# A second layer's dense width of 158 instead of 160, with the two tokens between as a gathered set of their own

## The chip, the cores and the metric

The kernel runs on one core of a Trainium2 chip. The metric is the device time of one execution in microseconds. A measurement gives the times of several runs and their median, and one more execution is recorded by the hardware profiler. Its trace counts from the first instruction to the last; that stretch is called the span.

The engines are called as the profile calls them: PE is TensorE (matmuls; PEld is its weight load), DVE is VectorE, ACT is ScalarE, POOL is GpSimd, SP is SyncE. DMA transfers are issued from queues of SP, ACT and POOL and carried by 16 DMA engines.

## The reference

The program is a trunk of two layers over 256 tokens of 1024 numbers. A layer first mixes tokens (projections, attention, convolution, gating) and then runs a retrieval over 16,384 single-neuron experts, which is what the change touches:

```python
q = (t @ w_pq).reshape(T, PEER_HEADS, 2, PEER_HALF)
...                                   # two top-16 searches over 128 keys, then 16 of the pairs per head
u = expert_down[experts]              # 8 heads x 16 = 128 rows of 1024 per token
act = gelu(einsum('td,thkd->thk', t, u))
wgt = gate * act
vv = expert_up[experts]               # the same 128 rows of the other table
y = einsum('thk,thkd->td', wgt, vv)
```

Each token uses 128 of the 16,384 experts. Both tables are 64 MB of float32 for each layer.

## The kernel before

**Two ways for a token.** For the first T tokens of a layer the kernel does not gather. It multiplies the whole table with them: the down table goes through PE in 128 chunks of 128 experts (8 matmuls of 128x128 weights by T columns each, L403), gives the dots of all experts with all T tokens, and these are masked by a matrix of gates that is zero where a token did not pick an expert. The up table then goes through PE in the same 128 chunks (L1225), into four PSUM banks named `acc`. These are the dense tokens, and T is `DENSE = (168, 160)` for the two layers.

The other TS = 256 - T tokens (88 and 96) are done from gathered rows. One indirect DMA (L1128, POOL) fetches 128 rows of the table, one row of 4 KB to each partition, 512 KB in all; here this is called a row step. A token needs 128 rows, one row step's worth, but the rows of one step belong to several tokens.

**Sets.** The gathered tokens are split into sets of m tokens, m a power of two. In a set of m, partition p holds token p mod m, and the 128 picks of each token are spread over 128/m partitions and m steps. So a set of m tokens needs m steps in the down half and m in the up half, and TS tokens need TS steps in each half, however they are split. `token_sets` gives offset and size of each: 64, 16, 8 in the first layer and 64, 32 in the second. Each set has a 128x1024 tile in `spots`: first its tokens' inputs, repeated over the partitions (`R_DX`), and later its weighted sum of up rows (`R_SUM`). There are four such tiles; those that are no set's serve as staging rows, one of them first holding the inputs before they are spread (`R_DROW`).

**The steps of a set.** `dot_spread` copies the inputs of set 0 into all partitions; `spread_inputs` (L1109) broadcasts those of the other sets from DRAM, 512 KB for each set. `spread_picks` (L1093) brings the picks of set 0 into `pairs`, and `spread_rest` (L1097, L1102) those of the others, two small DMAs for a set. `where` (L1113, DVE) makes row indices of them. Then `fetch` (L1128) issues row steps from POOL as long as a staging row is free; `dot` (L1138, DVE) multiplies a down row with the inputs and sums it, which frees the row for the next `fetch`; `add_row` (L1151 for a set's first row, else L1153, DVE) adds an up row times its weight to the set's sum. At the end `fold_set` (L1233, PE) adds the sums of the 128/m partitions of each token into the columns of `acc` behind the dense ones, eight matmuls for a set with a constant matrix `fold` of m columns. A set that is finished early is folded between chunks, one fold for each of eight chunks, starting 8 chunks after its last add stands in the order (`early_folds`); the last set is folded in and behind the last chunk.

**What sets the order.** From the expert stage on, the program is recorded in the order of the code (`manual_schedule`), so each engine does its instructions in that order and waits where an operand is late. The down loop takes a chunk on PE for each i and hangs the rest on i: gate groups of four tokens (`compare` L1161 on DVE, `factors` L1171 to L1177 on ACT, `gate_mm` L1187 on PE), the row steps, and after a start a fixed rate of dots per chunk (`DOT_RATE`, 0.92 in the second layer). The up loop spreads what is left of the dots and all adds over chunks 4 to 124. The dense weights come on the queues of SP and ACT into a ring of five units of 1 MB, one unit for two chunks; the row steps come on POOL's queue. All three share the 16 DMA engines.

**Rows.** In the second layer the staging rows are one tile of `spots`, the arena at 108, 80 and 84, `R_DROW` from chunk 7, for a time the places of chunks that were loaded ahead, two more after the start, one that is kept, and in the up half four more.

Of the kernel before, what the change touches and what calls it, by code (L numbers as in the profile page):

```python
# [40 lines left out]
PLAN1 = ((5, 'qk_sums k_norm'), (6, 'v_tok'), (7, 'lg10 exp'), (8, 'lg01 lg00 sm00'), (10, 'lg11'), (11, 'sm01 cz'), (12, 'sg'), (13, 'pt00 pt01 sm10 pv0'), (14, 'inv0 ao0 cy pt10'), (15, 'sm11 pt11 inv1 gs4 pv1 as0 ao1 gn4 mix'), (16, 'as1 an0'), (17, 'an1 sqrt'), (20, 'gs6 gn6'))  # L41
G_LAST = 124
OUT_AT = (3, 5, 6, 7)
DENSE = (168, 160)
QUEUE_LAG = 4
PICKS_LAG = 2
LOWER_LAG = 1
# [27 lines left out]

def token_sets(n):

    out, off = [], 0
    for m in (64, 32, 16, 8):
        if n & m:  # L80
            out.append((off, m))
            off += m
    assert off == n and len(out) <= 3
    return out


@with_exitstack
def hybrid_trunk(ctx: ExitStack, tc: tile.TileContext, x_in, c_in, vec_in, w_ada, w_first, w_in, w_out, w_pq,
# [48 lines left out]
    def region(at, *shape):  # L137
        n = 1
        for s in shape:
            n *= s  # L140
        v = flat[:, at:at + n]
        if len(shape) == 2:
            v = v.rearrange("p (a b) -> p a b", b=shape[1])
        elif len(shape) == 3:
            v = v.rearrange("p (a b c) -> p a b c", b=shape[1], c=shape[2])
        return v
# [908 lines left out]
    def experts(layer, rest):  # L1055

        T = DENSE[layer]
        TS = S - T
        SETS = token_sets(TS)
        NG = T // 4  # L1060
        acts = flat[:, :P * T].rearrange("p (i t) -> p i t", t=T)
        R_WHERE, R_DOTS = (region(127 * S, 2, TS)[:, n, :] for n in range(2))
        onehots = {}
        spots = work.tile([P, 4, D], F32, name="spots", tag="hh", bufs=1)
        R_DX = R_SUM = [spots[:, n, :] for n in range(len(SETS))]
        R_DROW = spots[:, 3, :]
        beyond = [region(at * S, D) for at in (80, 84) if at * S >= P * T]
        passing = []
        free = deque([spots[:, n, :] for n in range(len(SETS), 3)] + [region(108 * S, D)] + beyond)
        held = {}  # L1070
# [119 lines left out]

        def gate_use(g, ps, done):
            v = ps.rearrange("p (t i) -> p i t", t=4)
            a = acts[:, :, 4 * g:4 * g + 4]
            if done < 128:
                nc.scalar.activation(a[:, done:], v[:, done:], AF.Copy, scale=1.0 / GATE_SCALE)  # L1195
            if done:
                nc.vector.scalar_tensor_tensor(a[:, :done], a[:, :done], 1.0 / GATE_SCALE, v[:, :done],  # L1197
                                               op0=OP.mult, op1=OP.mult)
# [95 lines left out]
        gdone = 0  # L1294
# [6 lines left out]
        for i in range(128):  # L1301
# [4 lines left out]
            while waiting:  # L1306
                g, gp = waiting.pop(0)
                gate_use(g, gp, 2 * pair)
                gdone = g + 1
            if j == 1:  # L1310
                tdone = 4 * gdone
                pend.append((pair, gelu(pair, ps, tdone), tdone))
                if len(pend) > 1:
                    act_use(*pend.popleft())
# [203 lines left out]
```

## Time and profile before

| what | value |
|---|---|
| median of 3 runs | 1545.63 us (1544.82 to 1546.74) |
| the profiled execution | 1544.97 us |
| its span | 1543.3 us |
| mean granted PE clock | 0.998 |
| second layer's expert stage, down half | about 961 to 1256 us |
| second layer's expert stage, up half | about 1256 to 1537 us |
| HBM read | 563.50 MB |

A row of a timeline reads: start, duration, engine, line, operation, written tile <- read tiles, shapes, count, and in brackets how long the engine stood idle before it and what ended that. PE shows each float32 matmul as two records, so 16 records are one chunk. Durations of matmuls overlap; the distance between the starts is the pace. In the table of stretches each engine has its busy time and, in brackets, its instructions; then come the granted clock, the mean busy share of the 16 DMA engines (it can exceed 1 slightly) and what they moved.

### The profile page before, as it was taken

How to read it: one execution, taken by the hardware profiler on the slowest of the kernel's cores; microseconds unless marked ns; L12 is line 12 of the kernel's file. 1: busy time of each engine (PE TensorE's matmuls, PEld its weight loads, DVE VectorE, ACT ScalarE, POOL GpSimd, SP SyncE). 2: the span in 40 equal slices, each digit the busy share in tenths (PEclk: the TensorE clock that was granted, in tenths of full speed). 3: DMA queues.
4: the chain of work that ended last, by engine and by line, in shares of the span. 5: the costliest groups of instructions: out<-in, count | busy, mean ns of one | idle time of the engine just before them, and what ended most of it. 6: DMA issues, size and time to landing. Idle time of an engine off the chain costs nothing.

```text
span 1543.3 us, 28519 instructions
## 1 busy us (share of the span) xinstructions
PE 1527.7 (99%) x11244; PEld 1494.3 (97%) x11244; DVE 1000.2 (65%) x2249; ACT 478.7 (31%) x1380; POOL 503.2 (33%) x424
## 2 busy tenths in 40 slices
PE   8999999999999999999999999999999999999998
PEld 6879999999999999999999899999999999999998
DVE  7787879677687544444467578797777764443435
ACT  2256322466564000000036663234656620000000
POOL 0000125344334433443300002154344444444542
PEclk9999999999999999999999999999999999999999
DMA  9998299999999999999985573999999999999996
GB/s 387 386 362 319 93 312 380 422 422 422 422 422 420 420 422 423 422 424 423 422 319 169 170 257 107 280 409 423 421 423 423 422 422 423 423 423 423 424 422 283
DMA packets 122120, 570.65 MB, mean 370 GB/s; under 512 B 14292, under 2 KB 14820, under 8 KB 89986
## 3 DMA queue, kind: packets, MB, share of 16 engines
q1 hardware_dynamic: 48818, 240.54, 39.7%
q0 software_dynamic: 55744, 202.36, 32.6%
q10 hardware_dynamic: 17424, 125.93, 19.7%
q8 instruction: 88, 1.44, 0.3%
q14 instruction: 46, 0.38, 0.1%
HBM read 563.50 MB, written 4.09 MB: 368 GB/s over the span
## 4 chain that ended last, share of the span: by engine, by line
PE 84%; DMA 10%; DVE 3%; issue 1%; ACT 1%; POOL 0%; DVEq 0%; ACTq 0%; SPq 0%; POOLq 0%
PE acc L1225 37%; PE ch L403 28%; DMA arena<-in_down_rows,arena 5%; DMA spots<-in_down_rows,arena 3%; PE ch L405 2%; PE ch L406 2%; PE ch L407 2%; PE g L1187 2%; PE ch L494 1%; DVE raw L256 1%; PE g L999 1%; PE acc L405 1%; PE acc L407 1%; PE acc L406 1%; DMA raw<-in_w_ada 1%
## 5 line engine op out<-in xcount | busy, mean ns | idle before, releaser
L1225 PE MATMUL acc<-arena,raw 128*128 128x168 f32 (+1 forms) x4096 | 577.0, 303 | 0.0
L1225 PEld LDWEIGHTS acc<-arena,raw 128*128 128x128 f32 x4096 | 570.8, 190 | 0.0
L403 PE MATMUL ch<-arena,raw 128*128 128x168 f32 (+2 forms) x3808 | 564.3, 307 | 0.6 <-issue 0.6
L403 PEld LDWEIGHTS ch<-arena,raw 128*128 128x128 f32 x3808 | 539.3, 190 | 7.6 <-issue 3.9
L1153 DVE SCALAR_TENSOR_TENSOR spots<-arena,spots 128x1024 f32<-128x1024 f32 x154 | 197.8, 1285 | 263.3 <-DMA arena<-in_up_rows,arena 262.0
L1128 POOL DMA_INDIRECT arena<-in_up_rows,arena x159 | 216.6, 1362 | 283.8 <-DMA arena<-in_up_rows,arena 196.8
L1128 POOL DMA_INDIRECT arena<-in_down_rows,arena x147 | 177.0, 1204 | 223.3 <-DVE arena L1138 177.2
L1138 DVE SCALAR_TENSOR_TENSOR arena<-arena,spots 128x1024 f32<-128x1024 f32 x147 | 177.6, 1220 | 47.8 <-DMA arena<-in_down_rows,arena 46.0
L1171 ACT ACTIVATE arena<-arena,parts 128x128 f16<-128x128 f16 x164 | 64.6, 394 | 107.2 <-DVE arena L1161 85.1
L434 ACT ACT_TABLE_LOAD x6 | 7.7, 1283 | 247.9 <-PE acc L1225 247.8
L405 PE MATMUL ch<-hh,hi 128*128 128x256 f32 x288 | 82.6, 289 | 2.0 <-DVE arena L525 1.9
L406 PE MATMUL ch<-hh,lo 128*128 128x256 f32 x288 | 81.8, 284 | 0.0
L407 PE MATMUL ch<-hh,hi 128*128 128x256 f32 x288 | 81.8, 284 | 0.0
L1204 ACT ACTIVATE arena<-ch 128x336 f32<-128x336 f32 (+32 forms) x122 | 42.1, 346 | 123.7 <-PE ch L403 109.5
L1197 DVE SCALAR_TENSOR_TENSOR arena<-arena,g 128x336 f32<-128x336 f32 (+30 forms) x82 | 40.3, 492 | 49.6 <-ACT arena L1195 47.8
L256 DVE SCALAR_TENSOR_TENSOR raw<-raw,arena 128x1024 f32<-128x1024 f32 x48 | 58.4, 1221 | 12.2 <-DMA raw<-in_w_ada 12.1
L1128 POOL DMA_INDIRECT spots<-in_down_rows,arena x37 | 42.1, 1138 | 73.2 <-DVE spots L1138 54.7
L309 DVE TENSOR_TENSOR lo<-raw,hi 128x1024 fp32r<-128x1024 f32 x42 | 51.1, 1224 | 22.1 <-ACT hi L316 19.2
L1175 ACT ACTIVATE arena<-arena,parts 128x128 f16<-128x128 f16 x164 | 63.4, 387 | 0.0
L1173 ACT ACTIVATE arena<-arena,parts 128x128 f16<-128x128 f16 x164 | 63.4, 386 | 0.0
L1177 ACT ACTIVATE arena<-arena,parts 128x128 f16<-128x128 f16 x164 | 63.4, 386 | 0.0
L403 PE MATMUL ch<-arena 128*128 128x168 f32 (+1 forms) x448 | 63.0, 303 | 0.0
(239 smaller groups left out, 1754.9 us busy)
## 6 DMA issues: line engine op xcount, KB each, us to landing
raw<-in_up SPq DMA_DIRECT2D x64, 1024.0 KB
raw<-in_up ACTq DMA_DIRECT2D x64, 1024.0 KB
raw<-in_down SPq DMA_DIRECT2D x58, 1024.0 KB
raw<-in_down ACTq DMA_DIRECT2D x56, 1024.0 KB
raw<-in_w_ada SPq DMA_DIRECT2D x48, 512.0 KB
aside<-in_w_ada SPq DMA_DIRECT2D x48, 512.0 KB
raw<-in_w_pq SPq DMA_DIRECT2D x32, 512.0 KB
arena<-in_down SPq DMA_DIRECT2D x28, 512.0 KB
```

The lines of the kernel that those rows point to most:

```text
L256: nc.vector.scalar_tensor_tensor(raw, raw, 1.0, cact, op0=OP.mult, op1=OP.mult, accum_out=mods[layer][:, col:col + 1])
L403: nc.tensor.matmul(dst, hi[:, cols], k[0], start=start, stop=stop, **kw)
L405: nc.tensor.matmul(dst, hi[:, cols], k[0], start=start, stop=False, **kw)
L406: nc.tensor.matmul(dst, lo[:, cols], k[0], start=False, stop=False, **kw)
L407: nc.tensor.matmul(dst, hi[:, cols], k[1], start=False, stop=stop, **kw)
L1128: nc.gpsimd.indirect_dma_start(out=held[n], out_offset=None, in_=rows if n >= TS else down_rows[:, :], in_offset=bass.IndirectOffsetOnAxis ...
L1138: nc.vector.scalar_tensor_tensor(row, row, 1.0, R_DX[which(k)[0]], op0=OP.mult, op1=OP.mult, accum_out=R_DOTS[:, k:k + 1])
L1153: nc.vector.scalar_tensor_tensor(R_SUM[s], row, w, R_SUM[s], op0=OP.mult, op1=OP.add)
L1171: nc.scalar.activation(og[0][:, 0, i, :], oh[:, 0, i, :], AF.Copy, scale=parts[:, 0, t + i:t + i + 1])
L1173: nc.scalar.activation(og[1][:, 0, i, :], oh[:, 0, i, :], AF.Copy, scale=parts[:, 1, t + i:t + i + 1])
L1175: nc.scalar.activation(og[0][:, 1, i, :], oh[:, 1, i, :], AF.Copy, scale=parts[:, 0, t + 2 + i:t + 3 + i])
L1225: nc.tensor.matmul(acc[d // 2][:, (d % 2) * S:(d % 2) * S + T], u[:, d * P:(d + 1) * P], acts[:, i, :], start=i == 0 and d % 2 == 0, stop= ...
```

## The change

The second layer's width becomes 158. `token_sets` makes a set of two, if the number of gathered tokens has that bit, and puts it second: 98 tokens become sets of 64, 2 and 32. The first layer's 88 tokens give the same three sets as before. 158 is no multiple of four, so the number of gate groups is rounded up (it stays 40) and the last group uses two of its four columns. The second layer now has three tiles of `spots` as sets and one as `R_DROW`, so that the one that was a staging row from the start is none any more. Its gathered tokens take 98 row steps in each half instead of 96.

```diff
-DENSE = (168, 160)
+DENSE = (168, 158)
...
 def token_sets(n):
 
-    out, off = [], 0
-    for m in (64, 32, 16, 8):
-        if n & m:
-            out.append((off, m))
-            off += m
-    assert off == n and len(out) <= 3
-    return out
+    sizes = [m for m in (64, 32, 16, 8) if n & m]
+    if n & 2:
+        sizes.insert(1, 2)
+    assert sum(sizes) == n and len(sizes) <= 4
+    return [(sum(sizes[:k]), m) for k, m in enumerate(sizes)]
...
-        NG = T // 4
+        NG = -(-T // 4)
...
-        R_DROW = spots[:, 3, :]
         beyond = [region(at * S, D) for at in (80, 84) if at * S >= P * T]
+        R_DROW = spots[:, 3, :] if len(SETS) < 4 else beyond.pop()
...
             v = ps.rearrange("p (t i) -> p i t", t=4)
-            a = acts[:, :, 4 * g:4 * g + 4]
+            a = acts[:, :, 4 * g:min(4 * g + 4, T)]
+            v = v[:, :, :min(4, T - 4 * g)]
...
-                tdone = 4 * gdone
+                tdone = min(4 * gdone, T)
```

The lines of the changed program stand one or two higher than those of the program before. Three places show how the instructions move. The first is POOL at the beginning of the second layer's expert stage: `dot_in` takes the inputs to DRAM, the copies spots<-spots spread set 0, spots<-dot_in are the broadcasts of the other sets, pairs are the picks, and in_down_rows the row steps. Before:

```order
78 L1329 DMA dot_in_112<-spots 96x1024
79 L1088 DMA spots<-spots 64x1024 x2
80 L1109 DMA spots<-dot_in_112 128x1x1024
81 L1093 DMA pairs<-chosen 64x2x64 x2
82 L1128 DMA spots<-in_down_rows,arena 128x1024
83 L1128 DMA arena<-in_down_rows,arena 128x1024 x3
84 L1097 DMA pair_in_110<-chosen 96x256
85 L1102 DMA pairs<-pair_in_110 128x1x32 x2
```

Now:

```order
78 L1328 DMA dot_in_113<-spots 98x1024
79 L1086 DMA spots<-spots 64x1024 x2
80 L1107 DMA spots<-dot_in_113 128x1x1024 x2
81 L1091 DMA pairs<-chosen 64x2x64 x2
82 L1126 DMA arena<-in_down_rows,arena 128x1024 x4
83 L1095 DMA pair_in_111<-chosen 98x256
84 L1100 DMA pairs<-pair_in_111 128x1x2 x2
85 L1100 DMA pairs<-pair_in_111 128x1x32 x2
```

A second broadcast stands ahead of the picks, and two more small DMAs stand ahead of the fifth row step. The second place is DVE at the end of the down half and the beginning of the up half. Before:

```order
1105 L1215 TENSOR_TENSOR arena<-arena 128x320
1106 L1145 TENSOR_TENSOR arena<-arena,pairs 128x95
1107 L1138 SCALAR_TENSOR_TENSOR arena<-arena,spots 128x1024
1108 L1145 TENSOR_TENSOR arena<-arena,pairs 128x1
1109 L1151 TENSOR_SCALAR spots<-arena 128x1024
```

Now:

```order
1104 L1214 TENSOR_TENSOR arena<-arena 128x316
1105 L1143 TENSOR_TENSOR arena<-arena,pairs 128x95
1106 L1136 SCALAR_TENSOR_TENSOR arena<-arena,spots 128x1024 x3
1107 L1143 TENSOR_TENSOR arena<-arena,pairs 128x3
1108 L1149 TENSOR_SCALAR spots<-arena 128x1024
```

95 dots stand in the down half as before, and three in the up half instead of one. The third place is PE at the folds of set 0 in the second layer's up half. Before:

```order
2905 L1225 MATMUL acc<-arena,raw 128x160 x736
2906 L1233 MATMUL acc<-fold_103,spots 128x64
2907 L1225 MATMUL acc<-arena,raw 128x160 x8
2908 L1233 MATMUL acc<-fold_103,spots 128x64
2909 L1225 MATMUL acc<-arena,raw 128x160 x8
2910 L1233 MATMUL acc<-fold_103,spots 128x64
```

Now:

```order
2905 L1224 MATMUL acc<-arena,raw 128x158 x728
2906 L1232 MATMUL acc<-fold_103,spots 128x64
2907 L1224 MATMUL acc<-arena,raw 128x158 x8
2908 L1232 MATMUL acc<-fold_103,spots 128x64
2909 L1224 MATMUL acc<-arena,raw 128x158 x8
2910 L1232 MATMUL acc<-fold_103,spots 128x64
2911 L1232 MATMUL acc<-fold_103,spots 128x2
2912 L1224 MATMUL acc<-arena,raw 128x158 x8
2913 L1232 MATMUL acc<-fold_103,spots 128x64
2914 L1232 MATMUL acc<-fold_103,spots 128x2
```

Eight folds of the set of two stand between chunks, six of them right behind folds of set 0, and the first fold of set 0 stands one chunk earlier than before.

## The prediction

> **What bounds the kernel now.** I read the page's first lines, then a table of stretches, the waits, and last the end of the program in order of time.
>
> ```profile
> span 1543.3 us, 28519 instructions
> PE 1527.7 (99%) x11244; PEld 1494.3 (97%) x11244; DVE 1000.2 (65%) x2249; ACT 478.7 (31%) x1380; POOL 503.2 (33%) x424
> GB/s 387 386 362 319 93 312 380 422 422 422 422 422 420 420 422 423 422 424 423 422 319 169 170 257 107 280 409 423 421 423 423 422 422 423 423 423 423 424 422 283
> ```
>
> TensorE (PE) looks like the bound. But it is busy 99% also where it just keeps up with others, so the share settles nothing. The table of stretches (PE, PEld, DVE, ACT, POOL busy, clock, DMA share, GB/s) for the second layer's expert stage:
>
> ```profile
> 994.00:1000.00 6.00, 6.00 (x46) 6.00 (x46) 6.00 (x42) 0.61 (x3) 4.16 (x5) 1.00 0.61 205
> 1011.00:1020.00 9.00, 9.00 (x68) 9.00 (x67) 8.66 (x21) 2.47 (x4) 7.40 (x6) 1.00 1.00 399
> 1020.00:1167.00 147.00, 146.34 (x1173) 144.61 (x1171) 110.20 (x211) 77.61 (x271) 59.27 (x55) 1.00 1.02 422
> 1167.00:1256.00 89.00, 88.94 (x724) 88.18 (x723) 68.21 (x125) 50.69 (x183) 43.97 (x36) 1.00 1.02 422
> 1256.00:1456.00 200.00, 200.00 (x1474) 200.00 (x1474) 86.77 (x74) 1.38 (x6) 94.27 (x68) 1.00 1.02 423
> 1456.00:1515.00 59.00, 59.00 (x439) 59.00 (x438) 25.15 (x20) 0.00 (x0) 27.14 (x19) 1.00 1.02 423
> 1523.00:1535.00 12.00, 12.00 (x91) 12.00 (x90) 9.78 (x8) 0.00 (x0) 0.00 (x0) 1.00 0.44 175
> ```
>
> From 1020 us until after 1515 us the DMA engines are full (share 1.02) at 422 to 423 GB/s, whatever PE does. PE and DMA are both at their limit, so the question is which is late at the end. The end, in order of time (start, duration):
>
> ```profile
> 1520.39 1.43 POOL L1128 DMA_INDIRECT arena<-in_up_rows,arena  x1 [1.06 <-DMA arena<-in_up_rows,arena]
> 1525.51 7.89 DVE L1153 SCALAR_TENSOR_TENSOR spots<-arena,spots 128x1024 f32<-128x1024 f32 x6 [0.40 <-DMA arena<-in_up_rows,arena]
> 1535.27 0.30 PE L1233 MATMUL acc<-fold,spots 128*128 128x32 f32 x2
> 1536.10 3.43 DVE L438 SCALAR_TENSOR_TENSOR arena<-acc,mod,arena 128x256 f32<-128x256 f32 x8 [2.71 <-PE acc L1233]
> ```
>
> The last gathered row has been added at 1525.51 + 7.89 = 1533.40 us; PE's first fold that needs the finished sum stands at 1535.27. So the chain gather, add, fold has only 1.9 us of room under PE. From that fold to the end are 1543.3 - 1535.27 = 8.0 us. The waits from 946 us on (total, times, longest) say what the adds wait for:
>
> ```profile
> DVE spots L1153 <- DMA arena<-in_up_rows,arena: 121.7, 73, 4.3
> POOL arena L1128 <- DVE arena L1138: 78.9, 46, 3.5
> ```
>
> VectorE (DVE) waits for rows, GpSimd (POOL) for row buffers that DVE empties. The bound of this chain is the bytes on full DMA engines. In the down half it already touches PE once, through a gate that stood behind a dot on DVE:
>
> ```profile
> 1165.67 0.28 PE L1187 MATMUL g<-arena 128*128 128x128 f16 x2
> 1166.43 1.10 PE L1187 MATMUL g<-arena 128*128 128x128 f16 x6 [0.48 <-ACT arena L1171]
> ```
>
> **Term 1, what PE gains.** The chain of waits shows 16 records, one weight chunk, at width 168 (first layer), then a fold and a chunk at width 160, and a fold of 8 columns:
>
> ```profile
> 731.20 2.34 PE acc L1225 x16
> 797.14 0.12 PE acc L1233 x2
> 1461.01 0.17 PE acc L1233 x2
> 1461.18 2.23 PE acc L1225 x16
> ```
>
> Eight columns are 0.11 us, two are 0.0275 us. The second layer has 256 chunks: 7.0 us less. The set of two adds eight folds, each with a full weight load; I price them as the 8-column one, 8 x 0.12 = 1.0 us (below 8 x 0.17 = 1.4; not nothing, since 8 columns cost nearly what 64 do). The gate groups stay 40. Net on PE: 6.0 us less.
>
> **Term 2, what DMA gains in work.** Two more tokens are two more columns of indices in the down half and two in the up half: four gathers of 128 rows of 4 KB, 2.10 MB. On engines that are full at 422 GB/s this is 4.97 us. They cannot hide earlier: the queue is full from 1020 us to the tail. They would cost nothing only if something else left the queue; the weights stay as many bytes. A faster PE only draws them sooner and leaves the gathers less meanwhile.
>
> **Term 3, a later start of the gathers.** With three sets, GpSimd issues one more broadcast of 512 KB into the same queue, ahead of the DMAs that bring the picks (L1093) to the indices (L1113). The sizes of a broadcast (L1109) and of a copy before it (L1088), and the same place in the first layer, which has three sets already, and in the second, which has two:
>
> ```profile
> spots<-dot_in POOLq DMA_DIRECT2D x3, 512.0 KB
> spots<-spots POOLq DMA_DIRECT2D x4, 256.0 KB
> 203.15 1.17 POOL L1109 DMA_DIRECT2D spots<-dot_in  x2 [6.19 <-DMA dot_in<-spots]
> 212.93 1.20 POOL L1093 DMA_DIRECT2D pairs<-chosen  x2 [8.61 <-DVE arena L887]
> 224.93 0.20 DVE L1113 TENSOR_SCALAR arena<-pairs 128x64 uint32<-128x64 f32 x1 [7.61 <-DMA pairs<-chosen]
> 236.69 2.32 POOL L1102 DMA_DIRECT2D pairs<-pair_in  x4 [5.27 <-DMA pair_in<-chosen]
> 970.42 0.74 POOL L1109 DMA_DIRECT2D spots<-dot_in  x1 [5.82 <-DMA dot_in<-spots]
> 980.21 1.20 POOL L1093 DMA_DIRECT2D pairs<-chosen  x2 [9.05 <-DVE arena L887]
> 993.94 0.19 DVE L1113 TENSOR_SCALAR arena<-pairs 128x64 uint32<-128x64 f32 x1 [9.34 <-DMA pairs<-chosen]
> 1005.63 1.45 POOL L1102 DMA_DIRECT2D pairs<-pair_in  x2 [5.30 <-DMA pair_in<-chosen]
> ```
>
> From the broadcast's issue to the indices it is 21.8 us with two broadcasts and 23.5 us with one. So the low bound is no delay. For the high bound: in the 23.5 us the queue brings the broadcast and most of two copies of 256 KB, 1 MB; half as much again is 11 us. I take 3 us, nearer the first layer's row, because its scheme is the one that comes. Then four small DMAs in place of two, 2.32 - 1.45 = 0.9 us more on POOL. Behind both stand all gathers, and DVE, which waits in L1113 with the rest of its sorting behind it. In those 3.9 us the weights use part of the engines:
>
> ```profile
> raw<-in_down SPq DMA_DIRECT2D x58, 1024.0 KB
> 1127.75 4.56 PE L403 MATMUL ch<-arena,raw 128*128 128x160 f32 x32
> 1132.61 4.56 PE L403 MATMUL ch<-arena,raw 128*128 128x160 f32 x32
> ```
>
> One such transfer, two chunks, per 4.86 us is 216 GB/s. What is lost is 3.9 x (422 - 216) / 422 = 1.9 us of queue time, paid at the end since the queue is full after.
>
> The Trainium skill (DMA: Bandwidth & Descriptors, the section on why a DMA increments its semaphore by 16 and not by 1, and its rules for kernel authors) says that a transfer with a leading broadcast of c copies runs on at most c of the 16 engines. By it the set of 32 (4 copies) has sat on four engines with 32 rows each, and the set of two (64 copies) adds 8 rows to every engine, a quarter more: at most (993.94 - 980.21) / 4 = 3.4 us, an estimate from that page, and the sum below would be 1551.2 instead of 1551.0. The trace's totals cannot show single engines.
>
> **Term 4, buffers and DVE.** One staging row becomes the new set's sum, so fewer rows circulate. I cost it at nothing: the first layer has three sets and fewer rows, and its slices are as full (the GB/s row of the page: 420 to 424 in both layers). If that cover failed, the queue would show gaps below 422. DVE has four more row operations of 1.3 us, and waits 121.7 us for rows in this stage, so they hide, except in the tail without weights: there the adds follow at 7.89 / 6 = 1.315 us against 1.24 us per row by bytes. About four more rows fall into that tail: 0.3 us.
>
> **The sum.** Last add: 1533.40 + 4.97 + 1.9 + 0.3 = 1540.6; the fold right after it, at 1540.7 against 1535.27, and 8.0 us to the end: span 1548.7, 5.4 us longer. The profiled execution took 1544.97 us, the median of the runs is 1545.63; I add to the median: **1551.0 us**.
>
> Would PE be there in time? Before 1167 us its gain is void, since the gate behind the dots has no room and the gathers start later (1.9 us more stall). After that, 35 down chunks at 2.43 us and 127 up chunks give 162 x 0.0275 = 4.4 us, less 1.0 us of folds. There is one more place to wait, set 0's first fold:
>
> ```profile
> 1446.99 1.28 DVE L1153 SCALAR_TENSOR_TENSOR spots<-arena,spots 128x1024 f32<-128x1024 f32 x1 [1.23 <-DMA arena<-in_up_rows,arena]
> 1456.05 0.33 PE L1233 MATMUL acc<-fold,spots 128*128 128x64 f32 x2
> 1461.56 1.28 DVE L1153 SCALAR_TENSOR_TENSOR spots<-arena,spots 128x1024 f32<-128x1024 f32 x1 [1.28 <-DMA arena<-in_up_rows,arena]
> ```
>
> That sum is done at 1448.27, 7.8 us ahead. The fold moves one chunk earlier (2.2 us) and PE comes 1.4 us sooner (120 chunks' gain of 3.3 less 1.9 of stall), while the add comes about 4.2 rows later (two rows, 0.8 MB or 1.6 rows for the start, 0.6 for weights drawn sooner), at 2.9 us a row 12 us. PE would wait up to 8 us; while it waits no weights are drawn and the rows come about twice as fast, so some 3 to 4 us. It then reaches the end's fold near 1537, still ahead of 1540.7. Waits of PE thus change where the time shows, not the end.
>
> **The rivals.**
>
> *PE's gain shows (7%).* If the gathers had room, the time would be 1545.63 - 6.0 = 1539.6. For it: PE waits named by the profile are near nothing. Against: 1.9 us of room at the end, and 4.97 us of bytes into a queue without gaps.
>
> *No later start (18%).* If the new broadcast rides beside the others as in the first layer, terms 2 and 4 remain: add end 1538.7, 3.5 us longer, 1549.1. This is decided at L1113, at 993.94 or later. It lies at the border of what can be told.
>
> *A much later start (12%).* If all copies of two rows come slowly, 11 us and 0.9: 11.9 x 206 / 422 = 5.8 us in place of 1.9, 9.3 us longer, 1554.9.
>
> *The start takes the bytes up (6%).* The stretch 994 to 1000 us moves 205 GB/s only. If the new order filled it, 6 x 217 GB/s = 1.3 MB or 3.1 us would be won back and the start not lost: about 1546. Against: the indices come before the gathers, and nothing makes them earlier.
>
> **How the numbers follow.** The forecast has 57%, its own range 1549 to 1553. About 0.2% (3.1 us) is what a measurement of this kernel can tell from no change. Slower: 57 + 12 + 10 of the 18 = 0.78, rounded down; same: 8 + 6, with the rounding 0.15; faster: 0.07. The range, 1547 to 1556, leaves out the faster case, most of the fourth rival and the end of the third.
>
> **What would show it.** The lines move up by one or two. Right: the first index step of the second layer waits about 12 us for the picks, starting near 997; 16 records of a chunk take 2.20 us; DMA stays at 422 GB/s to about 1525; the last add ends near 1540.6, and PE waits at folds, first near 1453 and again at the end. Wrong: the last add before 1537, folds without a wait, or stretches after 1020 us below 415 GB/s, which would mean that the missing row buffer starves the queue and the time is above the forecast.

## The result and the profile after

The changed kernel takes 1561.13 us (median; 1558.27 to 1562.28), the kernel before 1546.1 us in all its runs beside it. The ratio is 1.0096, 95% interval 1.0083 to 1.0109: some 15 us slower, where 5.4 us were forecast and 1556 was the end of the range. The profiled execution took 1561.06 us. All ratios below are to the kernel before, run beside.

The span, from the page of the profile of the changed kernel:

```profile
span 1559.4 us, 28567 instructions
```

The table of stretches (PE, PEld, DVE, ACT, POOL busy, clock, DMA share, GB/s):

```profile
994.00:1000.00 6.00, 6.00 (x47) 6.00 (x46) 0.00 (x0) 1.21 (x6) 0.00 (x0) 1.00 0.34 123
1011.00:1020.00 9.00, 5.23 (x40) 4.99 (x38) 8.83 (x61) 1.84 (x3) 1.96 (x4) 1.00 0.80 307
1020.00:1167.00 147.00, 144.12 (x1133) 140.94 (x1134) 112.31 (x213) 73.97 (x258) 72.19 (x61) 0.99 1.01 414
1256.00:1456.00 200.00, 200.00 (x1492) 200.00 (x1491) 87.96 (x82) 1.83 (x7) 94.65 (x69) 1.00 1.02 423
1456.00:1515.00 59.00, 52.08 (x373) 51.84 (x372) 32.16 (x26) 0.00 (x0) 31.60 (x26) 0.91 1.02 420
1523.00:1535.00 12.00, 12.00 (x92) 12.00 (x91) 3.82 (x4) 0.00 (x0) 3.90 (x3) 1.00 1.02 426
```

Two stretches have changed in PE's column: 1011 to 1020 (9.00 to 5.23 us busy) and 1456 to 1515 (59.00 to 52.08). In both PE now stands still, which it did not do before. From 994 to 1000 us, where 205 GB/s flowed, it is 123. The kernel loses at the start of the gathers and at the folds.

**The start.** The second layer's first steps on POOL and DVE, in order of time; the set of two is among the four L1100 DMAs:

```profile
981.03 1.23 POOL L1091 DMA_DIRECT2D pairs<-chosen  x2 [7.29 <-DVE arena L885]
1000.55 0.20 DVE L1111 TENSOR_SCALAR arena<-pairs 128x64 uint32<-128x64 f32 x1 [15.13 <-DMA pairs<-chosen]
1018.04 2.65 POOL L1100 DMA_DIRECT2D pairs<-pair_in  x4 [11.06 <-DMA pair_in<-chosen]
1020.99 1.44 POOL L1126 DMA_INDIRECT spots<-in_down_rows,arena  x1 [0.30 <-issue]
```

The fifth row step before, the first one behind the picks of the other sets:

```profile
1007.39 1.01 POOL L1128 DMA_INDIRECT arena<-in_down_rows,arena  x1 [0.30 <-issue]
```

The picks of set 0 take 1000.55 - 981.03 = 19.5 us from issue to index step; before, 993.94 - 980.21 = 13.7. Then the round trip of the other sets' picks is late too: POOL waits 11.06 us for `pair_in` where it waited 5.30. The fifth row step starts 1020.99 - 1007.39 = 13.6 us later.

**PE's first new wait.** The changed kernel on ACT and PE:

```profile
1018.01 0.31 ACT L963 ACTIVATE arena<-arena 128x128 f32<-128x128 f32 x1 [8.59 <-DVE arena L962]
1020.24 14.96 PE L401 MATMUL ch<-arena,raw 128*128 128x158 f32 x97 [4.01 <-ACT arena L1203]
```

And the same instruction of ACT before:

```profile
1011.39 0.31 ACT L965 ACTIVATE arena<-arena 128x128 f32<-128x128 f32 x1 [2.20 <-DVE arena L964]
```

DVE stood 15.13 us in L1111 with the rest of its sorting behind it. ACT, which works in order, stood 8.59 us in an exponential that needs this sorting, and behind that stood the Gelu (L1203) that frees the PSUM bank for PE's next chunk. So a late index made PE idle for 4.01 us, by way of DVE's sorting and ACT's Gelu, neither of which uses the rows.

**The folds and the end.** PE's waits in the second layer (total, times, longest), then PE and DVE in order of time, all of the changed kernel:

```profile
PE acc L1232 <- DVE spots L1151: 6.9, 1, 6.9
PE ch L401 <- ACT arena L1203: 4.0, 1, 4.0
PE g L1185 <- ACT arena L1169: 2.1, 4, 0.6
```

```profile
1263.68 4.59 PE L1224 MATMUL acc<-arena,raw 128*128 128x158 f32 x33
1466.19 0.69 PE L1232 MATMUL acc<-fold,spots 128*128 128x64 f32 x2 [6.92 <-DVE spots L1151]
1466.67 4.53 PE L1224 MATMUL acc<-arena,raw 128*128 128x158 f32 x16
1470.99 0.53 PE L1232 MATMUL acc<-fold,spots 128*128 128x64 f32 x2
1473.88 0.50 PE L1232 MATMUL acc<-fold,spots 128*128 128x64 f32 x4
1474.24 2.39 PE L1224 MATMUL acc<-arena,raw 128*128 128x158 f32 x16
1538.94 7.89 DVE L1151 SCALAR_TENSOR_TENSOR spots<-arena,spots 128x1024 f32<-128x1024 f32 x6 [1.21 <-DMA arena<-in_up_rows,arena]
1551.36 0.30 PE L1232 MATMUL acc<-fold,spots 128*128 128x32 f32 x2
```

The last add ends at 1538.94 + 7.89 = 1546.83 us. PE comes to the end's fold only at 1551.36, without a wait. So the adds have 4.5 us to spare, and PE is last. The forecast had it the other way round. From that fold to the end it is 1559.4 - 1551.36 = 8.0 us, as before.

### The profile page after: what moved, and what is told of

Read it like the earlier page. It is cut to its first block, busy times and chain, and to the rows that moved or that the text cites. A ratio compares the mean times of both kernels' runs of the same rounds, so it can differ in the third digit from the quotient of the medians.

```text
span 1559.4 us, 28567 instructions
## 1 busy us (share of the span) xinstructions
PE 1530.9 (98%) x11260; PEld 1494.8 (96%) x11260; DVE 1005.2 (64%) x2257; ACT 477.2 (31%) x1380; POOL 505.3 (32%) x431
## 4 chain that ended last, share of the span: by engine, by line
PE 56%; DMA 21%; issue 12%; POOL 7%; DVE 3%; ACT 1%; SPq 0%; POOLq 0%; ACTq 0%; DVEq 0%
PE acc L1224 24%; PE ch L401 16%; DMA arena<-in_up_rows,arena 12%; POOL arena L1126 6%; DMA arena<-in_down_rows,arena 4%; PE ch L403 2%; PE ch L404 2%; PE ch L405 2%; DMA raw<-in_w_ada 2%; DMA spots<-in_down_rows,arena 2%; PE ch L492 1%; POOL spots L1126 1%; PE g L997 1%; PE acc L403 1%; PE acc L405 1%
## 5 line engine op out<-in xcount | busy, mean ns | idle before, releaser
L1151 DVE SCALAR_TENSOR_TENSOR spots<-arena,spots 128x1024 f32<-128x1024 f32 x162 | 208.1, 1284 | 271.2 <-DMA arena<-in_up_rows,arena 270.7
L1126 POOL DMA_INDIRECT arena<-in_up_rows,arena x168 | 226.6, 1349 | 289.5 <-DMA arena<-in_up_rows,arena 210.5
L1126 POOL DMA_INDIRECT arena<-in_down_rows,arena x159 | 188.3, 1184 | 263.1 <-DVE arena L1136 212.1
L1136 DVE SCALAR_TENSOR_TENSOR arena<-arena,spots 128x1024 f32<-128x1024 f32 x159 | 193.1, 1222 | 72.2 <-DMA arena<-in_down_rows,arena 72.0
L1203 ACT ACTIVATE arena<-ch 128x336 f32<-128x336 f32 (+42 forms) x122 | 41.7, 343 | 121.5 <-PE ch L401 113.4
L254 DVE SCALAR_TENSOR_TENSOR raw<-raw,arena 128x1024 f32<-128x1024 f32 x48 | 58.5, 1223 | 13.6 <-DMA raw<-in_w_ada 13.6
L401 PEld LDWEIGHTS ch<-arena 128*128 128x128 f32 x448 | 62.1, 190 | 0.0
```

Of the source, the lines that this page charges most:

```text
L401: nc.tensor.matmul(dst, hi[:, cols], k[0], start=start, stop=stop, **kw)
L1126: nc.gpsimd.indirect_dma_start(out=held[n], out_offset=None, in_=rows if n >= TS else down_rows[:, :], in_offset=bass.IndirectOffsetOnAxis ...
L1136: nc.vector.scalar_tensor_tensor(row, row, 1.0, R_DX[which(k)[0]], op0=OP.mult, op1=OP.mult, accum_out=R_DOTS[:, k:k + 1])
L1151: nc.vector.scalar_tensor_tensor(R_SUM[s], row, w, R_SUM[s], op0=OP.mult, op1=OP.add)
```

## The experiments

The theory: the broadcast of the new set stands ahead of the picks, the late indices make the whole stage late and stop PE in the down half, and PE's wait at set 0's first fold is not won back. The rivals: only the bytes of the four more row steps count; the missing staging row starves the queue; the place of the set of two in the line does harm.

### The set of 32 spread by four DMAs, in the changed kernel

```diff
                 src = dot_in[layer][off:off + n, :]
+                if n == 32:
+                    for h in range(P // n):
+                        nc.gpsimd.dma_start(R_DX[s][h * n:(h + 1) * n, :], src)
+                    continue
```

The same 512 KB; only the form of the transfer differs.

> The changed kernel, with the inputs of the second layer's set of 32 brought by four DMAs of 32 partitions instead of one DMA with four copies. Late start theory (the changed kernel is slow above all because its row steps begin 13.6 us later, behind a broadcast that sits on few DMA engines): the picks land well before 995 us instead of 1000.6, the fifth row step starts 10 us or more earlier than 1021, the 4 us stall of PE near 1016 is gone, and the time is 1545 to 1551 us. Bytes theory (the four row steps, 5 us of a full queue, and the waits of PE that follow from them are the loss; the start matters little): at most 3 us less than the changed kernel, 1558 to 1561 us.

Measured: 1552.8 us, ratio 1.0041 (1.0026 to 1.0055). Its first steps, PE's long wait, its last add and its end's fold:

```profile
980.56 1.20 POOL L1091 DMA_DIRECT2D pairs<-chosen  x2 [6.60 <-DVE arena L885]
988.35 0.20 DVE L1115 TENSOR_SCALAR arena<-pairs 128x64 uint32<-128x64 f32 x1 [3.40 <-DMA pairs<-chosen]
1003.14 2.64 POOL L1100 DMA_DIRECT2D pairs<-pair_in  x4 [4.81 <-DMA pair_in<-chosen]
1457.89 0.69 PE L1236 MATMUL acc<-fold,spots 128*128 128x64 f32 x2 [7.42 <-DVE spots L1155]
1529.54 7.89 DVE L1155 SCALAR_TENSOR_TENSOR spots<-arena,spots 128x1024 f32<-128x1024 f32 x6 [0.89 <-DMA arena<-in_up_rows,arena]
1541.75 0.30 PE L1236 MATMUL acc<-fold,spots 128*128 128x32 f32 x2
```

The picks take 7.8 us instead of 19.5, the other sets' picks are waited for 4.81 us instead of 11.06, PE's 4 us wait in the down half is gone, and 8.3 us of the 15 come back. That lies between the two ranges on record, nearer to that of the late start. Not all of the 8.3 us are the change's own: the same edit also helps the kernel before (a later experiment). The wait at set 0's first fold stays (7.42 us), and PE is again last: 1541.75 against 1529.54 + 7.89 = 1537.43.

### Set 0's fold eight chunks later, in the changed kernel

```diff
-FOLD_AFTER = 8
+FOLD_AFTER = 16
```

> The changed kernel with early folds 16 chunks behind a set's last add instead of 8. If the 6.9 us wait of PE at set 0's first fold and the slow chunks behind it (2.8 us) set the end, the wait is gone and the end comes as much earlier as the adds allow: the last add ended at 1546.8, it may come 1 to 2 us later since the weights are drawn without a pause, and 8.1 us follow: a span of 1555.5 to 1557, 1557 to 1559 us measured, with PE waiting at the last folds instead. If PE alone were the bound, 9.7 us less, 1551. If the wait only moved in time, the same 1561.

Measured: 1557.92 us, ratio 1.0069 (1.0052 to 1.0086): 3.2 us below the changed kernel by the medians, 4.2 by the ratios, with intervals that just touch. The profiled execution was the slowest of the four, 1561.86 us. The tail of this kernel, two groups of adds and PE at the end's fold:

```profile
1539.85 1.28 DVE L1151 SCALAR_TENSOR_TENSOR spots<-spots,arena 128x1024 f32<-128x1024 f32 x1
1541.17 9.21 DVE L1151 SCALAR_TENSOR_TENSOR spots<-arena,spots 128x1024 f32<-128x1024 f32 x7
1550.43 0.63 PE L1232 MATMUL acc<-fold,spots 128*128 128x32 f32 x2 [6.54 <-DVE spots L1151]
```

PE doesn't wait at set 0's fold any more, but 6.54 us at the end, for adds that follow each other without a gap. The wait has moved, and most of it is paid again: the tail is then bound by DVE. Waiting there also makes the tail itself longer: the fold's two records take 0.63 us instead of 0.30, and from the fold to the end of the span it is 1560.2 - 1550.43 = 9.8 us instead of 8.0, at a granted clock of 0.50.

### Only a second broadcast, in the kernel before

```diff
+            if len(SETS) == 2:
+                src = dot_in[layer][64:66, :]
+                src = bass.AP(tensor=src.tensor, offset=src.offset, ap=[[0, 64]] + list(src.ap))
+                nc.gpsimd.dma_start(spots[:, 2, :], src)
```

The tile that it fills is taken out of the staging rows of the second layer. No row step is added, and nobody reads the tile.

> The kernel before, with only a broadcast of two rows over all partitions added ahead of the other broadcast in the second layer, into the tile of spots that was a staging row (which no row step uses any more). Width, sets and row steps stay. Late start theory: this alone makes the picks land 3 to 7 us later and costs 3 to 8 us, 1549 to 1554. Bytes theory: 0.5 MB in a stretch where the DMA engines are not the end's bound, 0 to 1.2 us, 1546 to 1547.5.

Measured: 1550.69 us, ratio 1.0023 (1.0008 to 1.0037). Its picks, its index step and its fifth row step:

```profile
979.56 1.22 POOL L1093 DMA_DIRECT2D pairs<-chosen  x2 [7.90 <-DVE arena L887]
998.43 0.20 DVE L1117 TENSOR_SCALAR arena<-pairs 128x64 uint32<-128x64 f32 x1 [14.48 <-DMA pairs<-chosen]
1017.53 1.01 POOL L1132 DMA_INDIRECT spots<-in_down_rows,arena  x1 [0.30 <-issue]
```

18.9 us from picks to indices, and the fifth row step 10.1 us later than before. PE stands 2.63 us here, again behind ACT's Gelu (L1208). So one more broadcast in that place, with the tile that it takes, makes a late start without any other work, and it costs some 4 us (1.2 to 5.7 by the interval).

### One staging row less, in the kernel before

```diff
-        free = deque([spots[:, n, :] for n in range(len(SETS), 3)] + [region(108 * S, D)] + beyond)
+        free = deque([spots[:, n, :] for n in range(len(SETS), 3) if layer == 0] + [region(108 * S, D)] + beyond)
```

> The kernel before with one staging row less in the second layer, as in the changed kernel, and nothing else. If the missing row is no cost (term 4 of the prediction): 1545.5 to 1547. If it starves the queue: above 1549, with stretches after 1020 us below 415 GB/s.

Measured: 1547.12 us, ratio 1.0001 (0.9992 to 1.0011). By its time the row is worth nothing that can be told, 1.7 us at most. But its profile shows something else:

```profile
1009.99 1.45 POOL L1102 DMA_DIRECT2D pairs<-pair_in  x2 [8.96 <-DMA pair_in<-chosen]
1011.75 1.01 POOL L1128 DMA_INDIRECT spots<-in_down_rows,arena  x1 [0.30 <-issue]
```

From picks to indices it is 13.7 us, as before, and yet POOL waits 8.96 us for the other sets' picks instead of 5.30, and the fifth row step is 4.4 us late. So of the 10.1 us in the experiment before, the 998.43 - 993.94 = 4.5 us at the index step are the broadcast's; the rest may be due to the missing row too, though this is one execution. No run has the second broadcast with the row kept.

### Both: four DMAs and the later fold, in the changed kernel

```diff
-FOLD_AFTER = 8
+FOLD_AFTER = 16
...
+                if n == 32:
+                    for h in range(P // n):
+                        nc.gpsimd.dma_start(R_DX[s][h * n:(h + 1) * n, :], src)
+                    continue
```

> The changed kernel with both edits: the set of 32's inputs by four DMAs (1552.8 us alone) and early folds 16 chunks behind (1557.9 alone, 3.2 less than the changed kernel). If the late start and the wait at set 0's first fold are separate losses, they add up: 1549 to 1550.5, with PE waiting at the last folds for the adds of four more row steps. If the fold's wait is only a sign of the late bytes, nothing more than e1: 1552 to 1553. If PE's narrower chunks show once both are gone: below 1545.

Measured: 1552.82 us, ratio 1.0030 (1.0011 to 1.0050): no gain over the four DMAs alone that can be told. Its end's fold:

```profile
1538.72 0.64 PE L1236 MATMUL acc<-fold,spots 128*128 128x32 f32 x2 [5.65 <-DVE spots L1155]
```

The two gains don't add up, which was the second of the three cases on record. Once the start is early, the later fold only carries PE's wait to the end: the fold comes 3.0 us sooner than with the four DMAs alone, but from there to the end it is 1548.4 - 1538.72 = 9.7 us instead of 8.0.

### The four DMAs in the kernel before

```diff
+                if n == 32:
+                    for h in range(P // n):
+                        nc.gpsimd.dma_start(R_DX[s][h * n:(h + 1) * n, :], src)
+                    continue
```

> The kernel before with the set of 32's inputs by four DMAs. If the broadcast's few DMA engines hold the picks back here too, the first row step starts 3 us or more earlier than 994.9, the waits of PE at the gates (1.8 us) go, and the time is 1543.5 to 1545.5. If the start has nothing to do with it: 1546 to 1547.

Measured: 1543.65 us, ratio 0.9974 (0.9961 to 0.9988): faster than both kernels. Its picks and its index step:

```profile
979.06 1.20 POOL L1093 DMA_DIRECT2D pairs<-chosen  x2 [7.34 <-DVE arena L887]
985.77 0.20 DVE L1117 TENSOR_SCALAR arena<-pairs 128x64 uint32<-128x64 f32 x1 [2.32 <-DMA pairs<-chosen]
```

6.7 us from picks to indices instead of 13.7. So the late start was there before, with a single broadcast, and the change made a bad place worse. It also parts the loss: with four DMAs in both kernels the change costs (1.0041 - 0.9974) x 1546 = 10.4 us, with one broadcast 14.8 us. The start that the change makes later is worth the difference, some 4.5 us, near the 3.6 us of the second broadcast alone. The four intervals leave this some 4 us either way. About two thirds of the loss are there with an early start as well.

### Width 158 without the last two tokens

```diff
-        TS = S - T
+        TS = (S - T) // 4 * 4
...
```

The expert work of the last two tokens is left out (the rest of the edit fits the transposes, the picks and the last fold to 96 tokens), so this is PE's gain with the row steps of before.

> Width 158 with 96 gathered tokens in the sets of 64 and 32 of the kernel before. The expert stage's work for the last two tokens of the second layer is left out (their columns get zeros). PE's chunks are narrower by two columns, row steps and broadcasts are those before. Bytes theory and the prediction: the gathers have 1.9 us of room under PE, so nearly all of PE's 7 us turns into waits at gates and folds: 1543.5 to 1546.5. If PE is the bound: 1539 to 1541.

Measured: 1546.23 us, ratio 0.9995 (0.9978 to 1.0012). What PE gains can't be told from nothing; the interval leaves 3.4 us of the 7.0 at most. PE waits 0.69 us for the adds at the end's fold. The same with the set of 32 spread by four DMAs:

```diff
-        TS = S - T
+        TS = (S - T) // 4 * 4
...
+                if n == 32:
+                    for h in range(P // n):
+                        nc.gpsimd.dma_start(R_DX[s][h * n:(h + 1) * n, :], src)
+                    continue
...
```

> Width 158, the expert work of the last two tokens left out, and the set of 32 spread by four DMAs. In the kernel before with that spread the end's fold came 2.4 us behind the last add, so PE was last there by that much. Theory: PE's narrower chunks now show up to that room: 1541 to 1543 us, and the changed kernel with the same spread (1552.8) lies 10 to 12 us above, 5.0 of it bytes. Rival (PE's gain is worth nothing in any start): 1543.7 within the scatter, and the adds meet the end's fold.

Measured: 1542.57 us, ratio 0.9975 (0.9965 to 0.9985), which is the 0.9974 of the kernel before with four DMAs. The median lies in the range that was expected if PE's gain shows, but by the ratios there is no gain, and PE now waits at its end's fold, which is the rival's sign:

```profile
1533.79 0.58 PE L1240 MATMUL acc<-fold,spots 128*128 128x34 f32 x2 [1.95 <-DVE spots L1157]
```

With the start early in both, the two tokens and their broadcast cost (1.0041 - 0.9975) x 1546 = 10.2 us. By the prediction's second term their bytes are 5.0 of these. With the two tokens PE comes to the end's fold 4.3 us behind the last add (1541.75 against 1537.43); here it waits for the adds. That would leave about 1 us. It is a sum of readings, though, and not a test: as the run with both edits showed, taking PE's lag away doesn't give it back.

### The set of two last in line

```diff
-        sizes.insert(1, 2)
+        sizes.append(2)
```

> The changed kernel with the sets in the order 64, 32, 2. Broadcasts, row steps and width stay, the set of 32 is folded early and the set of two last, set 0's folds stay where they are. If the place in line does not matter: 1559 to 1563. If the second place costs: below 1558.

Measured: 1562.32 us, ratio 1.0101 (1.0076 to 1.0126). Its place makes no difference that can be told. The order of the two broadcasts changes with it, and the picks are as late: 1001.05 - 981.83 = 19.2 us to the index step.

### The broadcasts behind the picks, in both kernels

```diff
             if i == INPUTS_AT:
-                spread_inputs()
                 free.append(R_DROW)
...
                         where(s)
                     known_to[0] = 2 * TS
                     fetch()
+                    spread_inputs()
```

> The changed kernel with the broadcasts of the inputs of sets 1 and 2 issued behind the index step of all sets, some 30 chunks later, in both layers; 1 MB moves from the start into the full queue, 2.4 us. Late-start theory: the first index step of the second layer stands 22 to 26 us after the issue of dot_in in place of 36.8, PE has no 4 us wait in the down half, and the time is 1549 to 1554 us. Rival (the picks are late because of the weights, or only the bytes count): index step after 33 us still, 1561 to 1564 us.

> The kernel before with the same move. Late-start theory: index step 20 to 25 us after the issue of dot_in in place of 30.9, the gain of the four-DMA spread (2.5 us) less at most the 1.2 us of the 512 KB in a full queue: 1543 to 1546 us. Rival (only bytes count): 1547 to 1549 us.

Measured: 1573.2 us, ratio 1.0162 (1.0131 to 1.0192), and 1564.56 us, ratio 1.0111 (1.0094 to 1.0127). Both far slower, and further off than the rivals said. Of the changed kernel so altered, the picks, the index step, one piece of the chain of waits (start, duration), the dot at its end, and PE's wait:

```profile
990.91 1.21 POOL L1091 DMA_DIRECT2D pairs<-chosen  x2 [16.18 <-DVE arena L885]
997.28 0.20 DVE L1111 TENSOR_SCALAR arena<-pairs 128x64 uint32<-128x64 f32 x1 [1.99 <-DMA pairs<-chosen]
1048.64 34.34 DMA arena<-in_down_rows,arena
1083.00 1.23 DVE L1136 SCALAR_TENSOR_TENSOR arena<-arena,spots 128x1024 f32<-128x1024 f32 x1 [18.11 <-DMA arena<-in_down_rows,arena]
PE g L1185 <- ACT arena L1169: 15.6, 2, 15.0
```

The step that the theory was about came out: 6.4 us from picks to indices. The price of the late broadcasts was wrong. The row step that was issued next behind them took 34.34 us; DVE waited 18.11 us for it, the gates behind that dot were late, and PE stood 15.0 us. The first layer, whose broadcasts are late as well here, lost before that: the second layer's picks are issued 990.91 - 981.03 = 9.9 us later than in the changed kernel. In the kernel before so altered the row step behind the one broadcast of 32 rows took as long, by the chain of waits:

```profile
1043.45 35.33 DMA arena<-in_down_rows,arena
```

### The set of 32 by four DMAs, and late, in the kernel before

Both edits together, the late place in the second layer only.

```diff
+                if n == 32:
+                    for h in range(P // n):
+                        nc.gpsimd.dma_start(R_DX[s][h * n:(h + 1) * n, :], src)
+                    continue
...
             if i == INPUTS_AT:
-                spread_inputs()
+                if layer == 0:
+                    spread_inputs()
...
                     known_to[0] = 2 * TS
                     fetch()
+                    if layer == 1:
+                        spread_inputs()
```

> The kernel before with the set of 32 of the second layer spread by four DMAs, and these issued late, behind the index step of all sets, in the full queue; the first layer as before. In the run before, the late broadcast of 32 rows stood some 35 us in the full queue, the row steps behind it with it, and the time was 1564.6 us. Theory (the shape does it: four copies sit on few of the DMA engines, the rows behind wait on those): no row step waits over 20 us, PE has no wait of several us at a gate in the second layer, 1543 to 1547 us. Rival (512 KB in a full queue cost this in any shape): PE waits 5 us or more at a gate near 1075 us, and the second layer's half of the loss stays, 1552 to 1557 us.

Measured: 1550.41 us, ratio 1.0014 (0.9997 to 1.0031), between the two expectations. Its picks, two row steps of its chain of waits, one issued shortly ahead of the four DMAs and one behind, and PE's longest waits at gates of the second layer:

```profile
981.90 1.21 POOL L1093 DMA_DIRECT2D pairs<-chosen  x2 [15.59 <-DVE arena L887]
1026.48 23.33 DMA arena<-in_down_rows,arena
1050.57 20.52 DMA arena<-in_down_rows,arena
PE g L1191 <- ACT arena L1175: 1.3, 2, 0.6
```

PE's stop at the gates is gone, though row steps still take over 20 us. That is not out of the way: the row steps in the same part of the chain of waits of the kernel before take 17 to 22 us. The first layers differ here, so the second layer is counted from the picks to the end of the span. For the one broadcast put late the picks are these:

```profile
989.28 1.21 POOL L1093 DMA_DIRECT2D pairs<-chosen  x2 [16.20 <-DVE arena L887]
```

With four DMAs in their old place it is 1540.7 - 979.06 = 561.6 us; with one broadcast, late, 1563.9 - 989.28 = 574.6; with four DMAs, late, 1548.6 - 981.90 = 566.7. The kernel before, one broadcast in the old place, has 1543.3 - 980.21 = 563.1. So the late place costs 11.5 us for one broadcast and 5.1 for four DMAs, and the shape is worth 7.9 us in the full queue and 1.5 in the old place. Each figure is from one execution, and the times of one kernel lie 3 to 5 us apart here, so the two small ones are not clear of the noise.

## Why the prediction was wrong, point by point

The direction was right. The chain that the prediction went by (gather, add, fold) grew as it said and more, the last add 6.2 us later than forecast, but it was not the last one: PE came 4.5 us behind it. The 8.0 us from the fold to the end held, because PE didn't wait there. The span came out 1559.4 - 1548.7 = 10.7 us above the forecast. The misses are two.

**Term 3, a later start: the step that failed first.** The prediction took 3 us for the indices, bounds 0 and 11, and 0.9 us more on POOL. The index step came 6.6 us later, inside these bounds. What no bound held is the second round trip: the picks of the other sets (`pair_in`), which follow the first four row steps, are waited for 5.8 us longer. With the four DMAs the wait is 4.81 us in the changed kernel and 7.13 us in that with the later fold too; with one row less and the index step as before it was 8.96 us. In the six profiles with the row kept it is 4.3 to 5.3 us, in the eight without it 4.5 to 11.3. So the late index and the missing row may both have a part in it. That these four row steps then meet a burst of weights is my reading of it and was not tried; the cause of this second delay stays open. POOL's four small DMAs take 2.65 us, 1.2 us more than two. In all, the fifth row step was 13.6 us late in place of 3.9. By the prediction's conversion, 206/422 of queue time for each us, the 9.7 us too few are 4.7 us. For the second broadcast alone it gives 10.1 x 206 / 422 = 4.9 us, where the ratio 1.0023 is 3.6 us; for the missing row 4.4 x 206 / 422 = 2.1 us, where the ratio 1.0001 leaves 1.7 at most. So it is about right, and rather too high. The nearest row that I chose was the wrong one: the first layer's two broadcasts are sets of 16 and 8, the second layer's are of 32 and 2, and a set of 32 in one broadcast is the slow shape, as the runs with four DMAs show.

**"Waits of PE change where the time shows, not the end": the step that failed second.** PE was to reach the end's fold near 1537, ahead of the adds. It came at 1551.36, 4.5 us behind them. PE's own account from 1535.27: the up half begins 1263.68 us; before it was this:

```profile
1256.11 4.10 PE L1225 MATMUL acc<-arena,raw 128*128 128x160 f32 x29
```

That is 7.6 us later, 4.0 of them the stall; PE's clock was at 0.50 behind that too, from 1022 to 1024 us. The wait at set 0's fold is 6.9 us; up to 8 was said. Then two chunks with their folds took 1473.88 - 1466.19 = 7.7 us. Before, the third fold stood here:

```profile
1460.85 0.33 PE L1233 MATMUL acc<-fold,spots 128*128 128x64 f32 x2
```

There the same work took 1460.85 - 1456.05 = 4.8 us. The 2.9 us more come with a slower clock after PE had stood still (the last section). The set of two adds eight folds: a pair takes 1474.24 - 1473.88 = 0.36 us, the single one 0.17, so eight are 1.5 us. The up half's narrower chunks give back 128 x 0.0275 = 3.5. Together 15.4 of the 16.1 us (1551.36 - 1535.27). The experiment with the later fold shows what this step is worth: 3 to 4 us where the start is late. Where the start is early the prediction's sentence holds in its effect only: PE is last there too, by 4.3 us, but the later fold gained nothing that can be told.

One reason is a cost that the prediction didn't have. It let PE wait for the adds at the end, from 1537 to 1540.7, and still counted 8.0 us from there. In the three runs in which PE waited 1.95 to 6.54 us at the end's fold, that stretch took 9.6 to 9.8 us. So even with PE ahead of the adds the forecast would have been some 1.7 us too low.

**The rest of the difference.** 4.7 us of start and 4.4 us of PE behind the adds leave 1.6 us, by which the adds are later still. The stretch 1020 to 1167 moved 414 GB/s instead of 422, 147 x 8 / 422 = 2.8 us of queue time, which more than covers it. All of it lies in the first 15 us: 280 GB/s from 1020 to 1026, 379 from there to 1035, and 422 after. That is right behind PE's stall, at its slow clock, and behind the late fifth row step (1020.99); which of these makes it was not tried. The prediction had named such a stretch below 415 as the sign of a starved queue for want of a row buffer. The sign came, but the row alone did not bring it in time: that kernel is no slower.

**Term 1, PE's gain: right, and worth nothing that can be told.** 1492 matmul records in the 200 us from 1256 where there were 1474, 1.2% more, is 0.026 us for a chunk of 2.17 us against 0.0275. With the two tokens' work left out the time does not move beyond the noise, neither with the start of the kernel before nor with the early one. The price of the eight folds, 1.0 us, was 0.5 us too low.

**Term 2, the bytes: consistent, not shown by itself.** In the two kernels with four DMAs the last add ends at 1530.34 us before and 1537.43 us with the change, 7.1 us later. The bytes, 5.0, the tail, 0.3, and the fifth row step, 1006.08 - 1003.08 = 3.0 us later at 206/422, 1.5, are 6.8. No run has the row steps without their folds.

**Term 4, the missing row: right in time**, 1.0001, though in that run's profile the second round trip was longer.

**The rivals.** The case that came is the much later start, given 12%, with 11.9 us of delay against 13.6 measured. Its way was another, since it put 11 us before the indices, where 6.6 came, and had no second round trip; and its 1554.9 us lacked what PE lost. That the start is not later, and that it takes the bytes up, is refuted by the index step at 1000.55 and the 123 GB/s from 994 to 1000 us; that PE's gain shows, by the two runs without the two tokens. Of the signs, the index step came later than the 997 us said, with 15.13 us of waiting instead of 12, the last add at 1546.83 instead of 1540.6, and PE waited at set 0's fold but not at the end.

**The rule of the Trainium skill** (DMA: Bandwidth & Descriptors, the section on why a DMA increments its semaphore by 16 and not by 1, and its rules for kernel authors), by which a transfer with a leading broadcast of c copies runs on at most c engines: the runs agree with it, though no trace shows single engines. The set of 32 has four copies; written as four transfers of 32 partitions its bytes are the same, and the picks behind it take 6.7 us instead of 13.7. The prediction mentioned it, worked 3.4 us out of it for the new set and let the sum go by another row. Measured was 5.8 us from picks to indices (19.5 against 13.7), and only 7.8 - 6.7 = 1.1 us where the set of 32 is out of the way. So the new broadcast costs that much only together with the old one, ahead of it as in the changed kernel or behind it as with the set of two last.

## What to carry to other kernels

Before a broadcast is put into a queue ahead of a small transfer that everything waits for, look at how the one already there is written: the same bytes as four transfers of 32 partitions brought these picks 7 to 12 us sooner, and gave a kernel faster than both. When something gets late at the head of a stage, follow each in-order engine that stands in that wait (here DVE, then ACT, then PE) and the next round trip behind it, since each is paid on top of the delay itself. A wait of the main engine ahead of its last work costs nothing only while the other chain is last by more than that wait and the slow work behind it; and a wait at the last work itself makes that work slower, here 9.7 us instead of 8.0.

## What the runs showed of the hardware that was not expected

A row step of 512 KB issued next behind a broadcast of four copies, on full DMA engines, took 34 to 35 us; the first three behind the same bytes in four transfers took 20.5 us at most, no more than the 17 to 22 us in the chain of waits of the kernel before. The median of the down row steps in the changed kernel, from issue to landing (last column, us):

```profile
arena<-in_down_rows,arena POOLq DMA_INDIRECT x159, 16.1
```

So one transfer can double the time of those behind it while the engines' mean share stays full. In the changed kernel with late broadcasts the share was 1.03 from 1060 to 1073 us, and only 326 GB/s came through. How these go together is open.

After a wait of 6.9 us PE ran at half its clock. The stretch behind set 0's first fold in the changed kernel (clock is the third column from the end):

```profile
1466.00:1471.00 5.00, 4.81 (x19) 4.81 (x20) 3.91 (x5) 0.00 (x0) 3.78 (x5) 0.50 1.00 390
1471.00:1474.00 3.00, 3.00 (x21) 3.00 (x21) 2.89 (x4) 0.00 (x0) 2.39 (x3) 0.83 1.03 418
```

Microsecond by microsecond the clock is 0.50 up to 1472 us and 0.98 in the next one. So PE ran at half speed for about 5.8 us from 1466.19 us on, and that alone is the 2.9 us. Shorter waits did it too. After the 2.63 us in the kernel with the second broadcast the clock was 0.59 and 0.55 (1019 to 1023 us). After the 1.95 us at the end's fold, with the last two tokens left out and four DMAs, it was 0.52 (1533.8 to 1536 us) and 0.50 (1536 to 1538 us). After 0.69 us, with one broadcast, it stayed at 1.00.

The Trainium skill (TensorE: Matmul & The Clock Gate, the section on what's actually happening) has the clock halved after an idle window of about 3.4 us, until about 3.4 us of activity. The traces agree with the half but not with the lengths: 1.95 us of waiting were enough, and the half lasted 5.8 us. By the page it costs some 1.7 us, an estimate from that page; 2.9 us were measured for the two chunks and their folds.
